# A hybrid attention and DeltaNet layer: the products P V of a head pair in one visit, the relative bias in float32r, and new stream delays

## The chip, the core and the metric

The kernel runs on one core of a Trainium2 chip. The metric is the device time in microseconds (us) of one execution; smaller is better. The engines are named as in the profile: PE (TensorE, matmuls and transposes), PEld (its weight loads), DVE (VectorE), ACT (ScalarE), POOL (GpSimd) and SP (SyncE, which issues most transfers).

## The reference

One decoder layer with 512 tokens and width 1024, all in float32. Eight heads of block-sparse attention and eight heads of a gated DeltaNet work side by side on one input projection; their outputs share one output projection; an MLP with a squared ReLU follows. Cut to what matters:

```python
h = rms_norm(x, pre_mix_norm)
proj = h @ w_in                       # 512x1024 by 1024x(3*512 + 3*512 + 512 + 16)
att_q, att_k, att_v, gdn_qkv, gdn_z, gdn_a, gdn_b = split(proj)

# attention, 8 heads of 64: own block of 256 keys (causal) and the past block
l = q k^T / 8 + rel_bias[:, rel_bucket(q_pos - k_pos)]     # -inf where not visible
p = softmax(l);  o_att = p v
# rel_bucket(d): d below 16, else 16 + log-spaced up to 31; rel_bias is 8 x 32

# gated DeltaNet, 8 heads of 64, chunks of 64 tokens
q, k, v = silu(causal_conv4(gdn_qkv)); q, k l2-normalised
u, w = triangular_solve(I + strict_lower(beta k k^T * decay), [beta v, beta k e^g])
for each chunk:                        # a scan over 8 chunks with a 64x64 state
    v_new = u - w S;  o = q S + (q k^T * decay) v_new;  S = S e^g_last + k^T v_new
o_gdn = rms_norm(o) * norm_w * silu(z)

x = x + rms_norm([o_att, o_gdn] @ w_out, post_mix_norm)
m = square(relu(rms_norm(x, pre_mlp_norm) @ w_up)) @ w_down     # 1024 -> 4096 -> 1024
out = x + rms_norm(m, post_mlp_norm)
```

## The kernel before, in words

**Arithmetic.** A float32 product of the projections is made from three float32r passes: each operand is split in a high part (`_h`, `_hi`: the value rounded to float32r) and the remainder (`_l`, `_lo`), and `mm3` issues high x high, high x low and low x high. Rows `ps_mm<-hT_h,w_hi`, `hT_l,w_hi`, `hT_h,w_lo` are such passes of 512 columns with the transposed, normed input `hT` and a chunk of `w_in`. A chunk `w_raw` comes by a transfer of SP (256 KB), ACT makes `w_hi` of it (L154), and POOL or DVE makes `w_lo` (L155). `LO_DVE = (26, 40)` names the chunks whose `w_lo` is DVE's.

**Streams and their order.** The front of the layer is written as generators: `projections` (the spine, whose items `k0 q0 x0 k1 ...` stand in the string `ORDER`; k, q, v, z are parts of the DeltaNet, x and y queries and keys of the attention, w the attention's values), `pre_norm`, `constants_in`, `bias`, `scalars`, `chunks(p)`, `inverse`, `scan`, `scores`, `values`, `finish_o(t)`, `weights_out`, `output` and others. A class `Weave` runs them. It keeps a virtual time `now` which each matmul advances by its columns / 2400 us (four times that in float32), and always continues the first stream, in rank order, whose start has come. A stream gives way with `yield wait["name"]` (so many us later) or `yield "mark"` (when another stream has set that mark). `WAIT` and `SINGLE` hold those delays, per name or per occurrence, `RANK` and `LEAD` the ranks and priorities, `START` some first starts. The order on PE is exactly the order in which the generators issue; the other engines' queues are set in issue order at first and by the tile scheduler later, with `LEAD` as priority. Each engine works through its own list in order, so PE waits where its next instruction's operand or bank is late. A second part, from the attention's end on (output projection, norm, MLP), follows.

**Banks.** PSUM has eight banks of 128x512, by tag: two `mm` (projections), three `g` (DeltaNet) and three `a` (attention). A row's `ps_a` is a bank of tag `a`.

**Attention.** The heads go in four pairs p = 0..3. `scores` (from L682) makes for each block of 128 queries, q = 3, 2, 1, 0, the scores of both heads in two `a` banks (`ps_a<-pt`), DVE adds the bias read from `E` and keeps the smallest (L708), ACT takes the exponential into `L` (L710) and sets the mark `row{p}{q}` later. The inverses of the row sums are copied to `R` (L715), with a mark `sums{p}`. `values` (L720 to L770) handles one pair after another. `block(k)` transposes the parts of `L` that belong to key block k on PE (L101, `ps_a<-ident,L`) into `a` banks and copies them to `ph` on ACT (L736). `product(k, P)` adds P V of that key block, two heads side by side on the PE columns (128x64 tiles, `ps_a<-ph,V`), into the bank `po`; key block k has 512 - 128 k columns, and each product is four records in the trace. The order in a pair is: block 3, take bank `po`, then block 2, product 3, block 1, product 2, product 1, block 0, the transposes of `R` into a bank `rb` (copied to `t` by ACT, L762), product 0, and the scaling. Between those steps the stream yields, so projection passes or DeltaNet work stand between.

**Relative bias.** `bias_in` (L197) loads a one-hot table `hot` (33 x 640: bucket by distance; row 32 is the mask row) and `rel_bias` into `rb` (33 x 8). `bias` (L651) multiplies them in float32 on PE in two matmuls (512 and 128 columns; `ps_a<-L,rb`), copies the 8 x 640 result with its sign changed into `es` and stores it to DRAM, from where `scores` reads each head's row as a sliding window.

**DeltaNet.** k and q go through a convolution on ACT and DVE (L409, L412, L416) and are transposed on PE (`ps_g<-ident,kraw`); sums of squares become rsqrt factors by a power on POOL (`rstd_of`, L188 and L192, tile `by`). `inverse` works on DVE, and `scan` joins it: the merge is two runs of 32x32 matmuls (`uap,NT` and `UT,uap`), then 64x64 ones (`UT,kB`), then eight scan steps (`S,LWQ`, `vn,kdec`, `vn,AT`). `finish_o(t)` norms a token tile's output and transposes it (`ps_g<-ident,ot`), and DVE scales it into `om` (L933). `weights_out` loads the 16 chunks `wo_raw` of the output projection; `output` uses them (`wo_h,mg_h`).

Of the kernel before, what the change touches and what calls it, by code (L numbers as in the profile page):

```python
# [85 lines left out]
def layer(ctx, tc, nc, x, w_in, w_v, w_ab, w_out, w_up, w_down, conv_w, a_log, dt_bias, gdn_norm_w, rel_bias,  # L86
          pre_mix, post_mix, pre_mlp, post_mlp, c_ident, c_mask, c_tri, c_ones, c_sel, c_su, c_hot, out):
    stt = nc.vector.scalar_tensor_tensor
    tt = nc.vector.tensor_tensor
# [4 lines left out]
    ctx.enter_context(tc.manual_schedule(engines={mybir.EngineType.PE}))

    def mm(o, l, r, **kw):
        nc.tensor.matmul(o, l, r, **kw)  # L97
# [97 lines left out]
    rel = []  # L195

    def bias_in():  # L197
        he = at.tile([128, 1280], FT, name="L")
# [3 lines left out]
        nc.vector.memset(rb, -1e30)
# [517 lines left out]
    def values():  # L720
        for p in range(4):
            yield f"row{p}3"
            yield "v"

            def block(k):
                w = 512 - 128 * k
                P = []
                for hs in (((0, 1),) if k > 1 else ((0,), (1,))):
                    tp = bank("a")
                    for i, hh in enumerate(hs):  # L730
                        for q in range(k, 4):
# [4 lines left out]
                    nc.scalar.copy(pt[:, :n], tp[:, :n])  # L736
# [25 lines left out]
            nc.scalar.copy(rs, rb)  # L762
# [771 lines left out]
```

## Time and profile before

| | us |
|---|---|
| median of 3 runs (lowest to highest) | 632.41 (632.14 to 632.89) |
| span of the profiled execution | 634.2 |
| PE busy | 622.9 |
| DVE, ACT, POOL busy | 443.7, 359.4, 157.9 |

The profiled execution's time is that span, 634.2 us; the runs without the profiler are the metric. In the profile's rows, a time is in us from the start of the span; `x4` counts records; `128*64 128x256` is a PE tile of 128 rows and 64 columns with 256 columns of moving data; `[0.29 <-ACT ph L736]` says that the engine had been idle 0.29 us and what ended that. A name in front of `<-` is written, those behind it are read. PE's matmuls overlap, so the step from one start to the next is what a matmul costs.

### The profile page before, as it was taken

How to read it: one execution, taken by the hardware profiler on the slowest of the kernel's cores; microseconds unless marked ns; L12 is line 12 of the kernel's file. 1: busy time of each engine (PE TensorE's matmuls, PEld its weight loads, DVE VectorE, ACT ScalarE, POOL GpSimd, SP SyncE). 2: the span in 40 equal slices, each digit the busy share in tenths (PEclk: the TensorE clock that was granted, in tenths of full speed). 3: DMA queues.
4: the chain of work that ended last, by engine and by line, in shares of the span. 5: the costliest groups of instructions: out<-in, count | busy, mean ns of one | idle time of the engine just before them, and what ended most of it. 6: DMA issues, size and time to landing. Idle time of an engine off the chain costs nothing.

```text
span 634.2 us, 11129 instructions
## 1 busy us (share of the span) xinstructions
PE 622.9 (98%) x4359; PEld 524.1 (83%) x4359; DVE 443.7 (70%) x635; ACT 359.4 (57%) x610; POOL 157.9 (25%) x197
## 2 busy tenths in 40 slices
PE   8999999999999999999999999999999999999995
PEld 6877777877876777688998999999998888888884
DVE  4456667599724464658665678878789888887776
ACT  6366586254387548654225586566765656665661
POOL 4346555500234343004212311111130320000001
PEclk9999999999999999999999999999999999999999
DMA  7222332422731112563488899999999999867503
GB/s 247 78 90 83 84 109 76 128 88 71 186 94 52 36 35 82 188 229 132 162 336 233 159 276 268 228 241 286 270 264 340 310 291 285 270 213 283 198 1 132
DMA packets 60629, 113.16 MB, mean 178 GB/s; under 512 B 15734, under 2 KB 35321, under 8 KB 60194
## 3 DMA queue, kind: packets, MB, share of 16 engines
q1 hardware_dynamic: 42876, 83.09, 37.8%
q0 software_dynamic: 17696, 29.36, 22.2%
q8 instruction: 34, 0.56, 0.3%
q14 instruction: 17, 0.14, 0.1%
q10 hardware_dynamic: 6, 0.00, 0.0%
HBM read 106.65 MB, written 35.15 MB: 224 GB/s over the span
## 4 chain that ended last, share of the span: by engine, by line
PE 91%; DVE 3%; DMA 2%; ACT 2%; POOL 1%; issue 0%; POOLq 0%; DVEq 0%; SPq 0%; ACTq 0%
PE ps_mm L97 46%; PE ps_g L97 26%; PE ps_a L97 16%; PE ps_a L101 2%; PE ps_g L101 1%; DMA wo_raw<-in_w_out 1%; DMA xx<-in_x 1%; DVE conv L412 1%; DMA w_raw<-in_w_in 0%; DVE wo_l L143 0%; POOL w_lo L155 0%; POOL oss L192 0%; DVE hT_l L131 0%; POOL by L192 0%; DVE xs L249 0%
## 5 line engine op out<-in xcount | busy, mean ns | idle before, releaser
L130 ACT CAST wdh<-wd 128x1024 fp32r<-128x1024 f32 x53 | 55.9, 1054 | 51.4 <-PE ps_mm L97 22.6
L131 DVE TENSOR_TENSOR u_l<-w,u_h 128x1024 fp32r<-128x1024 f32 x46 | 56.2, 1224 | 37.3 <-ACT u_h L130 37.1
L131 DVE TENSOR_TENSOR wdl<-wd,wdh 128x1024 fp32r<-128x1024 f32 x53 | 64.9, 1224 | 22.2 <-ACT wdh L130 22.1
L130 ACT CAST u_h<-w 128x1024 fp32r<-128x1024 f32 x46 | 47.9, 1046 | 56.8 <-DVE w L1177 15.6
L97 PE MATMUL ps_mm<-hT_h,w_hi 128*128 128x512 f32 (+1 forms) x192 | 79.4, 413 | 0.0
L97 PE MATMUL ps_mm<-hT_l,w_hi 128*128 128x512 f32 (+1 forms) x192 | 74.6, 388 | 0.3 <-DVE hT_l L131 0.3
L97 PE MATMUL ps_mm<-hT_h,w_lo 128*128 128x512 f32 (+1 forms) x192 | 74.5, 388 | 0.0
L155 POOL TENSOR_TENSOR w_lo<-w_raw,w_hi 128x512 fp32r<-128x512 f32 x40 | 51.8, 1297 | 77.2 <-ACT w_hi L154 67.4
L1210 POOL DMA_DIRECT2D d_T<-in_w_down x32 | 33.0, 1033 | 143.8 <-DMA d_T<-in_w_down 82.4
L154 ACT CAST w_hi<-w_raw 128x512 fp32r<-128x512 f32 x56 | 34.6, 620 | 52.9 <-PE ps_mm L97 17.5
L97 PEld LDWEIGHTS ps_mm<-hT_h,w_hi 128*128 128x128 f32 x192 | 37.1, 193 | 11.3 <-issue 4.8
L97 PE MATMUL ps_mm<-wdh,u_h 128*128 128x512 f32 x116 | 45.2, 390 | 0.0
L97 PE MATMUL ps_mm<-wdl,u_h 128*128 128x512 f32 x116 | 45.1, 389 | 0.0
L97 PE MATMUL ps_mm<-wdh,u_l 128*128 128x512 f32 x116 | 45.1, 389 | 0.0
L97 PEld LDWEIGHTS ps_mm<-hT_h,w_lo 128*128 128x128 f32 x192 | 37.2, 194 | 7.5
L97 PEld LDWEIGHTS ps_mm<-hT_l,w_hi 128*128 128x128 f32 x192 | 37.3, 194 | 6.0 <-DVE hT_l L131 0.6
L412 DVE SCALAR_TENSOR_TENSOR conv<-ps_mm,cw,conv 128x511 f32<-128x511 f32 (+2 forms) x36 | 26.8, 745 | 11.3 <-ACT conv L409 11.0
L131 DVE TENSOR_TENSOR u_l<-f,u_h 128x1024 fp32r<-128x1024 f32 x28 | 34.1, 1217 | 0.0
L708 DVE CUSTOM_DVE_ANT_0 L<-ps_a,E 128x512 f32<-128x512 f32 (+3 forms) x32 | 14.4, 489 | 23.9 <-PE ps_a L97 23.7
L97 PE MATMUL ps_g<-wdh,u_h 128*128 128x512 f32 x80 | 31.1, 389 | 0.0
L97 PE MATMUL ps_g<-wdl,u_h 128*128 128x512 f32 x80 | 31.1, 389 | 0.0
L97 PE MATMUL ps_g<-wdh,u_l 128*128 128x512 f32 x80 | 31.1, 389 | 0.0
(452 smaller groups left out, 1761.3 us busy)
## 6 DMA issues: line engine op xcount, KB each, us to landing
d_T<-in_w_down POOLq DMA_DIRECT2D x48, 512.0 KB, 11.6
wd<-d_T SPq DMA_DIRECT2D x32, 512.0 KB, 6.2
w<-in_w_up SPq DMA_DIRECT2D x28, 512.0 KB, 8.0
wd<-in_w_down SPq DMA_DIRECT2D x24, 512.0 KB, 7.7
w_raw<-in_w_in SPq DMA_DIRECT2D x46, 256.0 KB, 2.7
wo_raw<-in_w_out SPq DMA_DIRECT2D x16, 256.0 KB, 3.4
d_T<-d_T POOLq DMA_DIRECT2D x8, 512.0 KB, 12.7
xx<-in_x SPq DMA_DIRECT2D x4, 512.0 KB, 6.4
```

Of the source, the lines that this page charges most:

```text
L97: nc.tensor.matmul(o, l, r, **kw)
L101: nc.tensor.transpose(o, i, ident[:k, :k])
L130: nc.scalar.copy(hi, src)
L131: tt(lo, src, f32(hi), op=OP.subtract)
L154: nc.scalar.copy(hi, raw)
L155: (sub or tt)(lo, raw, f32(hi), op=OP.subtract)
L412: stt(c[:, s:], p[:, :512 - s], cw[:, ft, j:j + 1], c[:, s:], op0=OP.mult, op1=OP.add)
L708: nc.vector.tensor_tensor_reduce(out=l, in0=s[hh][:, :w], in1=Es[hh][:, w - 1::-1], scale=1.0, scalar=3e38, op0=OP.add, op1=OP.min, accum_ ...
L1210: nc.gpsimd.dma_start(d_T[t][k], block(b, second)[k], accum_op=OP.add, max_dma_last_dim=1024)
```

## The change

**P V.** In `values` a pair's four blocks are transposed first, k = 3, 2, 1, 0, each when its mark `row{p}{k}` has come; `ph` has 8 buffers instead of 4. Then come the transposes of `R`, the wait `pv0`, and only then the bank `po` and all four products in a row.

**Bias.** The constant `hot` is 128 x 640 with the table in rows 0 to 32 and again in 64 to 96, zero elsewhere; it is loaded after `rel_bias`. POOL casts it to float32r (`hot_r`, in the second buffer named `L`), ACT writes the high part of `rb` into rows 0 to 32 of `rs`, DVE the remainder into rows 64 to 96 (the rest is set to zero), so that one float32r pass sums high and low part. That preparation waits for the mark `h3` (the fourth token tile has been transposed) and the delay `bias`.

**Delays.** All tables have other numbers, `SINGLE` has many more entries, q1 and q2 and the order of v0 to v3 change places in `ORDER`, and `LO_DVE` is (33, 46). The counts of matmuls are the same but for the bias.

The diff (tables cut to a line or two):

```diff
-WAIT = {'h': 1.7, 'conv_k': 5.5, ..., 'wo': 0.97, 'wo_out': 17.6, ..., 'pv0': 1.53}
+WAIT = {'h': 0.99, 'conv_k': 5.48, ..., 'wo': 5.9, 'wo_out': 26.28, ..., 'pv0': 4.65, 'bias': 0.77}
...
-ORDER = "k0 q0 x0 k1 q1 q2 y0 k2 k3 z0 q3 x1 w0 v0 v1 v2 v3 y1 x2 y2 x3 y3 z1 z2 z3"
-LO_DVE = (26, 40)
+ORDER = "k0 q0 x0 k1 q2 q1 y0 k2 k3 z0 q3 x1 w0 v1 v3 v2 v0 y1 x2 y2 x3 y3 z1 z2 z3"
+LO_DVE = (33, 46)
...
     def bias_in():
         he = at.tile([128, 1280], FT, name="L")
-        hot, es = he[:33, :640], he[:8, 640:]
-        nc.sync.dma_start(hot, c_hot)
+        hot, es = he[:, :640], he[:8, 640:]
         rb = at.tile([33, 8], FT, name="rb", bufs=1)
         nc.vector.memset(rb, -1e30)
         nc.sync.dma_start(rb[:32], rel_bias)
-        return hot, es, rb
+        nc.sync.dma_start(hot, c_hot)
+        rs = at.tile([128, 8], FR, name="rs", bufs=1)
+        nc.vector.memset(f32(rs), 0.0)
+        return hot, es, rb, rs
...
     def bias():
-        hot, es, rb = rel
+        hot, es, rb, rs = rel
+        hot_r = at.tile([128, 1280], FT, name="L")[:, :640].bitcast(FR)
+        yield "h3"
+        yield wait["bias"]
+        nc.gpsimd.tensor_copy(hot_r, hot)
+        nc.scalar.copy(rs[:33], rb)
+        tt(rs[64:97], rb, f32(rs[:33]), op=OP.subtract)
         yield max(0, START[4] - weave.now)
         for a, b in ((0, 512), (512, 640)):
             pe = bank("a")
-            mm(pe[:8, :b - a], rb, hot[:, a:b], start=True, stop=True)
+            mm(pe[:8, :b - a], rs, hot_r[:, a:b], start=True, stop=True)
...
-                    pt = at.tile([128, 512], FT, name="ph", bufs=4)
+                    pt = at.tile([128, 512], FT, name="ph", bufs=8)
...
-            P = block(3)
-            po = bank("a")
+            P = {3: block(3)}
             for k in (2, 1, 0):
                 yield f"row{p}{k}"
-                if k > 0:
-                    N = block(k)
-                yield wait["pv"]
-                product(k + 1, P)
-                if k == 0:
-                    N = block(0)
-                P = N
+                P[k] = block(k)
             mark(f"turned{p}", wait["turned"])
...
             yield wait["pv0"]
-            product(0, P)
+            po = bank("a")
+            for k in (3, 2, 1, 0):
+                product(k, P[k])
```

What this does to the engines' lists is seen at three places. First, PE in pair 0, from the last transposes of `R` and `L` to the P V products; before, the products of key blocks 2 and 1 and their surroundings:

```order
L97 MATMUL ps_mm<-hT_h_83,w_lo 128x512
L97 MATMUL ps_a<-ph,V 64x256 x2
L97 MATMUL ps_mm<-hT_h_82,w_hi 128x512
L97 MATMUL ps_mm<-hT_l_84,w_hi 128x512
L97 MATMUL ps_mm<-hT_h_82,w_lo 128x512
L97 MATMUL ps_a<-ph,V 64x384 x2
L101 MATMUL ps_a<-ident,L 128x128 x8
L101 MATMUL ps_a<-ident,R_1042 128x128 x4
L97 MATMUL ps_mm<-hT_h_82,w_hi 128x512
```

After, the transposes:

```order
L97 MATMUL ps_mm<-hT_h_82,w_lo 128x512
L101 MATMUL ps_a<-ident,L 128x128 x20
L101 MATMUL ps_a<-ident,R_1069 128x128 x4
L97 MATMUL ps_mm<-hT_h_82,w_hi 128x512
L97 MATMUL ps_mm<-hT_l_84,w_hi 128x512
```

and, 21 projection passes later, the products:

```order
L97 MATMUL ps_mm<-hT_h_83,w_lo 128x512
L97 MATMUL ps_a<-ph,V 64x128 x2
L97 MATMUL ps_a<-ph,V 64x256 x2
L97 MATMUL ps_a<-ph,V 64x384 x2
L97 MATMUL ps_a<-ph,V 64x512 x2
L97 MATMUL ps_mm<-hT_h_82,w_hi 128x512
```

All 20 transposes of `L` and the four of `R` are now one group, and the four products another. Second, PE in pair 1, where the merge of the inverse, the P V products and the first scores of pair 2 (`ps_a<-pt`) meet; before:

```order
L97 MATMUL ps_g<-uap,NT 32x32 x64
L97 MATMUL ps_a<-ph,V 64x128 x2
L101 MATMUL ps_a<-ident,L 128x128 x6
L97 MATMUL ps_g<-UT,uap 32x32 x64
L97 MATMUL ps_a<-ph,V 64x256 x2
L97 MATMUL ps_a<-ph,V 64x384 x2
L101 MATMUL ps_a<-ident,L 128x128 x8
L97 MATMUL ps_g<-UT,kB 64x64 x16
L101 MATMUL ps_a<-ident,R_2025 128x128 x4
L97 MATMUL ps_a<-pt 128x512 x6
L97 MATMUL ps_g<-UT,kB 64x64 x16
L97 MATMUL ps_a<-ph,V 64x512 x2
```

After:

```order
L97 MATMUL ps_g<-uap,NT 32x32 x64
L101 MATMUL ps_a<-ident,L 128x128 x8
L101 MATMUL ps_a<-ident,R_2030 128x128 x4
L97 MATMUL ps_g<-UT,uap 32x32 x64
L97 MATMUL ps_a<-pt 128x512 x6
L97 MATMUL ps_a<-ph,V 64x128 x2
L97 MATMUL ps_a<-ph,V 64x256 x2
L97 MATMUL ps_a<-ph,V 64x384 x2
L97 MATMUL ps_a<-ph,V 64x512 x2
L97 MATMUL ps_g<-UT,kB 64x64 x16
```

The second 32x32 run has moved between the transposes of `R` and the scores, and the products have come together behind the scores. Third, POOL between its casts of the constants (`picks`) and the first power for k (`by`, L188 and L192); before:

```order
L386 CAST picks<-ident 128x128
L155 TENSOR_TENSOR w_lo<-w_raw,w_hi 128x512 x4
L188 TENSOR_SCALAR by_100<-ssq 128x4x2
L192 TENSOR_TENSOR by_100<-by_100,mhalf 128x4x2
L155 TENSOR_TENSOR w_lo<-w_raw,w_hi 128x512
```

After:

```order
L388 CAST picks<-ident 128x128
L658 CAST L<-L 128x640
L155 TENSOR_TENSOR w_lo<-w_raw,w_hi 128x512 x5
L188 TENSOR_SCALAR by_100<-ssq 128x4x2
L192 TENSOR_TENSOR by_100<-by_100,mhalf 128x4x2
L155 TENSOR_TENSOR w_lo<-w_raw,w_hi 128x512
```

The cast of the table (L658) has come in, and five chunks instead of four stand ahead of the power.

More of the change, by code (lines that the diff above doesn't have):

```diff
@@ L18 @@
 EPS = 1e-6
-WAIT = {'h': 1.7, 'conv_k': 5.5, 'k': 5.19, 'conv_q': 6.15, 'q': 2.1, 'conv_v': 11.0, 'v': 6.02, 'z': 2.87, 'ab': 0.1, 'g': 11.93, 'scalars': 4.76, 'r_in': 0.65, 'r_out': 4.45, 'kk': 2.71, 'kk_out': 14.43, 'gl': 3.13, 'qk': 3.88, 'va': 0.83, 'a': 5.81, 'row': 1.38, 'rows': 5.12, 'pv': 1.54, 'att': 1.17, 'inverse': 1.23, 'merge': 11.0, 'p1': 2.8, 'p2': 1.7, 'w': 2.33, 'vn': 1.0, 'state': 1.21, 'o_in': 3.96, 'o': 3.73, 'wo': 0.97, 'wo_out': 17.6, 'normed3': 7.6, 'normed': 11.21, 'n': 1.7, 'up': 1.9, 'sums': 2.64, 'turned': 0.5, 'pv0': 1.53}
@@ L22 @@
-SINGLE = {('h', 0): 0.05, ('inverse', 6): 2.02, ('state', 6): 3.71, ('row', 5): 0.98, ('inverse', 18): 0.05, ('inverse', 25): 0.05, ('vn', 7): 0.05, ('pv', 2): 0.1, ('h', 1): 0.05, ('turned', 0): 0.9, ('conv_k', 0): 4.12, ('normed', 0): 10.21, ('wo', 1): 1.97, ('conv_q', 0): 8.0, ('inverse', 16): 1.63, ('state', 1): 1.57, ('row', 6): 0.38, ('conv_v', 1): 8.5, ('conv_q', 2): 7.0, ('conv_k', 1): 5.1, ('o_in', 1): 4.36, ('kk', 2): 2.03, ('h', 2): 0.85, ('rows', 2): 6.66, ('vn', 1): 0.75, ('pv', 4): 2.77, ('inverse', 0): 0.61, ('rows', 0): 5.52, ('pv', 6): 2.0, ('rows', 4): 0.1, ('conv_v', 0): 14.3, ('kk_out', 0): 11.93, ('gl', 0): 5.63, ('inverse', 27): 0.23, ('row', 12): 2.48, ('state', 0): 0.21}
@@ L24 @@
-RANK = {'chunks': 1, 'inverse': 3, 'scan': 3, 'scores': 5, 'values': 5, 'finish_o': 2, 'take': 4}
-LEAD = {'chunks': 0, 'inverse': 100, 'scan': 100, 'scores': 0, 'values': 100, 'finish_o': 0, 'take': 200, 'take_a': 100}
+WAIT = {'h': 0.99, 'conv_k': 5.48, 'k': 5.65, 'conv_q': 5.41, 'q': 2.85, 'conv_v': 11.04, 'v': 2.5, 'z': 2.38, 'ab': 5.21, 'g': 7.58, 'scalars': 7.45, 'r_in': 0.22, 'r_out': 3.39, 'kk': 3.95, 'kk_out': 21.17, 'gl': 5.7, 'qk': 2.58, 'va': 0.38, 'a': 5.09, 'row': 2.47, 'rows': 5.12, 'pv': 1.45, 'att': 3.93, 'inverse': 0.05, 'merge': 7.32, 'p1': 3.55, 'p2': 0.79, 'w': 1.77, 'vn': 1.0, 'state': 2.54, 'o_in': 4.39, 'o': 3.11, 'wo': 5.9, 'wo_out': 26.28, 'normed3': 16.96, 'normed': 12.84, 'n': 2.52, 'up': 1.02, 'sums': 2.36, 'turned': 0.42, 'pv0': 4.65, 'bias': 0.77}
@@ new lines @@
+SINGLE = {('inverse', 6): 2.02, ('state', 6): 3.66, ('row', 5): 0.98, ('inverse', 25): 0.05, ('vn', 7): 0.14, ('pv', 2): 0.1, ('normed', 0): 10.24, ('wo', 1): 0.05, ('conv_q', 0): 8.69, ('inverse', 16): 1.63, ('state', 1): 1.57, ('row', 6): 0.33, ('vn', 1): 0.75, ('pv', 4): 2.77, ('inverse', 0): 0.93, ('rows', 0): 6.08, ('pv', 6): 2.0, ('rows', 4): 0.22, ('conv_v', 0): 14.23, ('kk_out', 0): 4.37, ('inverse', 27): 0.23, ('row', 12): 2.48, ('state', 0): 0.05, ('vn', 4): 0.05, ('g', 0): 11.27, ('n', 1): 2.8, ('row', 9): 4.41, ('inverse', 20): 1.09, ('state', 4): 1.35, ('inverse', 28): 4.43, ('rows', 7): 8.76, ('w', 2): 2.04, ('kk', 0): 2.54, ('normed3', 0): 8.63, ('n', 2): 1.44, ('state', 5): 2.54, ('r_in', 3): 1.83, ('w', 3): 2.33, ('scalars', 0): 4.74, ('rows', 5): 4.36, ('row', 3): 4.63, ('n', 0): 5.62, ('z', 3): 0.05, ('inverse', 3): 1.71, ('inverse', 9): 4.8, ('state', 2): 3.37, ('o_in', 1): 1.66, ('ab', 0): 1.72, ('inverse', 12): 1.27, ('o_in', 0): 2.04, ('sums', 0): 1.83, ('r_in', 0): 0.83, ('q', 3): 4.02, ('wo', 9): 2.75, ('rows', 11): 4.94, ('r_in', 2): 0.05, ('up', 1): 2.35, ('k', 0): 6.39, ('row', 13): 2.25, ('inverse', 21): 0.68, ('pv0', 2): 1.9, ('up', 6): 0.71, ('up', 2): 1.8, ('z', 1): 1.9, ('rows', 9): 5.32, ('rows', 6): 4.96, ('row', 15): 2.64, ('row', 1): 1.47, ('a', 0): 4.5, ('att', 2): 0.05, ('wo', 14): 10.37, ('wo', 13): 5.87, ('r_out', 2): 4.4, ('rows', 8): 4.94, ('v', 0): 14.25, ('conv_k', 3): 5.47, ('up', 0): 0.82, ('att', 1): 1.03, ('conv_q', 3): 4.72, ('normed', 1): 13.89, ('rows', 1): 6.91, ('inverse', 2): 0.05, ('k', 1): 4.72, ('turned', 0): 0.05, ('vn', 3): 1.16, ('q', 2): 3.48, ('pv0', 1): 4.89, ('q', 0): 2.14, ('o', 3): 4.07, ('k', 3): 5.87, ('up', 5): 2.84, ('wo_out', 0): 19.54, ('inverse', 10): 0.9, ('merge', 0): 10.2, ('v', 2): 12.67, ('w', 0): 1.68, ('inverse', 19): 1.66, ('pv0', 0): 4.39, ('wo', 2): 1.79, ('z', 0): 0.05, ('inverse', 24): 1.39, ('a', 3): 5.72, ('wo', 11): 3.51, ('rows', 3): 6.28, ('inverse', 14): 0.15, ('att', 0): 3.37, ('row', 10): 2.37, ('conv_k', 0): 8.86, ('v', 3): 14.13, ('normed', 2): 12.25, ('z', 2): 0.05, ('row', 2): 2.64, ('kk', 1): 4.01, ('wo', 12): 3.29, ('r_in', 1): 0.05, ('turned', 3): 0.69, ('q', 1): 2.97, ('att', 3): 6.62, ('v', 1): 8.52, ('up', 3): 0.37, ('wo', 4): 4.12, ('gl', 0): 4.0, ('vn', 6): 1.14, ('sums', 1): 0.05, ('inverse', 4): 0.32, ('row', 8): 1.29, ('k', 2): 6.9, ('h', 1): 2.19, ('row', 14): 2.55, ('n', 3): 0.68, ('inverse', 1): 0.05, ('wo', 5): 6.26, ('r_out', 1): 5.83, ('conv_v', 2): 10.65, ('r_out', 3): 4.33, ('inverse', 13): 0.05, ('state', 7): 2.1, ('h', 2): 1.08, ('o', 2): 3.63, ('w', 1): 1.57, ('conv_q', 2): 5.4, ('bias', 0): 0.23, ('a', 2): 4.78, ('p2', 0): 0.05, ('rows', 14): 5.33, ('turned', 1): 0.4, ('r_out', 0): 4.58, ('row', 7): 2.28, ('sums', 3): 1.81, ('o', 0): 2.87}
@@ L26 @@
+RANK = {'chunks': 2, 'inverse': 5, 'scan': 3, 'scores': 4, 'values': 4, 'finish_o': 1, 'take': 4}
+LEAD = {'chunks': 50, 'inverse': 50, 'scan': 50, 'scores': 200, 'values': 100, 'finish_o': 300, 'take': 300, 'take_a': 200}
 FILL = (6, 2)
 AT_X = (3, 5)
-START = (5.5, 9.7, 18.5, 13.8, 30, 15.0)
-ORDER = "k0 q0 x0 k1 q1 q2 y0 k2 k3 z0 q3 x1 w0 v0 v1 v2 v3 y1 x2 y2 x3 y3 z1 z2 z3"
-LO_DVE = (26, 40)
+START = (7.33, 8.64, 16.11, 13.39, 30.84, 13.77)
+ORDER = "k0 q0 x0 k1 q2 q1 y0 k2 k3 z0 q3 x1 w0 v1 v3 v2 v0 y1 x2 y2 x3 y3 z1 z2 z3"
@@ L1498, in constants @@
     bucket = np.where(d < 16, d, np.minimum(large, 31))
-    hot = np.zeros((33, 640), f)
-    hot[bucket, 127 + d] = 1
-    hot[32, :127] = 1
+    hot = np.zeros((128, 640), f)
+    for o in (0, 64):
+        hot[o + bucket, 127 + d] = 1
+        hot[o + 32, :127] = 1
     return {"c_ident": np.eye(128, dtype=f), "c_mask": np.where((n % 64)[:, None] <= np.arange(64), 0, -1e30).astype(f), "c_tri": upper.astype(f),
```

## The prediction

> **What bounds the kernel now.** I read the page's busy times, slices and chain first, then the list of waits of TensorE (PE), then the timeline round each place that the diff touches. The page's rows:
>
> ```profile
> span 634.2 us, 11129 instructions
> ...
> PE 622.9 (98%) x4359; PEld 524.1 (83%) x4359; DVE 443.7 (70%) x635; ACT 359.4 (57%) x610; POOL 157.9 (25%) x197
> ...
> PEclk9999999999999999999999999999999999999999
> ...
> PE 91%; DVE 3%; DMA 2%; ACT 2%; POOL 1%; issue 0%; POOLq 0%; DVEq 0%; SPq 0%; ACTq 0%
> ```
>
> PE is busy 98% of the span at full granted clock and is 91% of the chain that ended last. What shortens PE's own work or its waits shortens the time, and nothing else does. The stretches table splits the span at the start of the MLP's unbroken matmuls (columns: stretch, length, busy us and records of PE, PEld, DVE, ACT, POOL, then clock, DMA share, GB/s):
>
> ```profile
> 317.50:627.70 310.20, 310.16 (x1899) 279.43 (x1897) 246.88 (x236) 181.50 (x222) 47.68 (x60) 1.00 0.87 247
> ```
>
> There PE waits for nothing, and the diff leaves this order of matmuls as it was. The result is decided in the first 317 us. PE's waits (total, times, longest; the three below 0.7 us that belong to the first loads left out):
>
> ```profile
> PE ps_g L97 <- DVE rb L202: 1.1, 1, 1.1
> PE ps_g L101 <- DVE kraw L416: 1.0, 1, 1.0
> ...
> PE ps_g L101 <- DVE om L933: 0.4, 1, 0.4
> ...
> PE ps_a L101 <- ACT ph L736: 0.3, 1, 0.3
> PE ps_a L97 <- ACT t L762: 0.2, 1, 0.2
> ```
>
> So waits are short, some 2 us beyond the start. Most of what can be won is inside "busy".
>
> **Part 1: P V in one visit.** Pair 0 in the timeline (start, busy, engine, line, operation, count of records):
>
> ```profile
> 135.31 0.44 PE L97 MATMUL ps_a<-ph,V 128*64 128x128 f32 x4
> 135.68 0.88 PE L101 MATMUL ps_a<-ident,L 128*128 128x128 f32 x6
> ...
> 138.57 0.65 PE L97 MATMUL ps_a<-ph,V 128*64 128x256 f32 x4
> 139.16 0.50 PE L97 MATMUL ps_mm<-hT_h,w_hi 128*128 128x512 f32 x1
> 139.50 0.40 PE L97 MATMUL ps_mm<-hT_l,w_hi 128*128 128x512 f32 x1
> ...
> 140.06 0.87 PE L97 MATMUL ps_a<-ph,V 128*64 128x384 f32 x4
> 140.86 1.09 PE L101 MATMUL ps_a<-ident,L 128*128 128x128 f32 x8
> 142.24 0.55 PE L101 MATMUL ps_a<-ident,R 128*128 128x128 f32 x3 [0.29 <-ACT ph L736]
> ```
>
> Matmuls overlap, so I take starts, not durations. A product (four records) takes 0.37 us with 128 columns (135.31 to 135.68), 0.59 with 256, 0.80 with 384: 0.213 for each 128 columns and 0.157 once. The three projection passes between two visits take 0.90 (139.16 to 140.06). The same passes in an unbroken run, from the chain, and two products that already stand together in pair 1:
>
> ```profile
> 562.38 21.76 PE ps_g L97 x96
> ...
> 187.58 1.30 PE L97 MATMUL ps_a<-ph,V 128*64 128x256 f32 x8
> 188.81 1.09 PE L101 MATMUL ps_a<-ident,L 128*128 128x128 f32 x8
> ```
>
> 21.76 / 96 = 0.227 a pass, so three are 0.68; the way back costs 0.22. Two products of 256 and 384 columns take 1.23 = 5 x 0.213 + 0.165: the second pays nothing fixed. A visit costs 0.157 + 0.227 = 0.384 beyond its columns, whatever it holds.
>
> All products together are one group, 16 products of four records:
>
> ```profile
> L97 PE MATMUL ps_a<-ph,V 128*64 128x128 f32 (+3 forms) x64 | 11.8, 453 | 0.0
> ```
>
> Columns and records stay. Before, by the program's order, the 16 products make 13 visits of their own (pairs 0 to 3: 4, 3, 2, 4) and two stand next to the scan's S matmuls, which have the same 128x64 shape; one visit holds two. After, three pairs have one visit and pair 2's stands next to the S matmuls: 10 visits fewer, 10 x 0.384 = **-3.8 us**. Lower end, if leaving is paid anyway: 10 x 0.157 = -1.6. The blocks' transposes come in other groups (28 visits for 24); by 135.68 to 136.31, 0.63 for six, they cost little on entry: +0.1.
>
> [...]
>
> **Part 2: the bias in float32r.** Before (first two rows) and the nearest float32r matmuls of a narrow tile:
>
> ```profile
> 33.72 1.24 PE L97 MATMUL ps_a<-L,rb 33*8 33x512 f32 x4
> 34.89 0.66 PE L101 MATMUL ps_g<-ident,kraw 128*128 128x128 f32 x4
> ...
> 22.09 0.40 PE L97 MATMUL ps_g<-hT_h,abw 128*32 128x512 f32 x1
> 22.50 0.42 PE L97 MATMUL ps_g<-hT_l,abw 128*32 128x512 f32 x1
> 22.76 0.40 PE L97 MATMUL ps_g<-hT_h,abw 128*32 128x512 f32 x1
> 22.99 0.39 PE L97 MATMUL ps_g<-hT_l,abw 128*32 128x512 f32 x1
> ```
>
> Before: 34.89 - 33.72 = 1.17. After: 640 columns at 0.23 per 512 are 0.29, and entering cost 0.41 - 0.23 = 0.18 there: 0.47, so **-0.7** (ends -0.9 without the entry, -0.5 with 0.18 on leaving too). The cost beside PE: the hot table is 128 rows instead of 33, a longer transfer that SP now issues behind rel_bias; a cast of 128x640 on POOL; a 33x8 cast on ACT; a memset and a subtraction of a few elements on DVE. POOL's cast, from the row
>
> ```profile
> 27.42 2.52 POOL L155 TENSOR_TENSOR w_lo<-w_raw,w_hi 128x512 fp32r<-128x512 f32 x2 [5.35 <-ACT w_hi L154]
> ```
>
> is 2.52 / 2 x 640 / 512 = 1.6 us. POOL had idled 5.35 us before that row and the cast stands there, so 0. If the table's transfer were late, five w_lo would queue behind the cast and PE behind them: up to 1 us.
>
> **Part 3: the new delays.** They only matter where PE waited or will wait. (a) k1:
>
> ```profile
> 51.58 0.40 PE L97 MATMUL ps_mm<-hT_h,w_lo 128*128 128x512 f32 x1
> 52.98 0.66 PE L101 MATMUL ps_g<-ident,kraw 128*128 128x128 f32 x4 [1.00 <-DVE kraw L416]
> ...
> 41.83 1.65 POOL L192 TENSOR_TENSOR by<-by,mhalf 128x8 f32<-128x8 f32 x1
> 43.45 1.29 POOL L155 TENSOR_TENSOR w_lo<-w_raw,w_hi 128x512 fp32r<-128x512 f32 x1
> ```
>
> PE lost 1.40 - 0.23 = 1.17. The w_lo at 43.45 stood behind the 1.65 us power on POOL; now it is ahead of it, and the transposes stand three passes (0.68) later on PE. 1.65 + 0.68 covers 1.17: **-1.15** (ends -1.2 and 0). Late next is the power, which the preparation of the scan's chunks needs. (b) The scores of pair 2:
>
> ```profile
> 191.04 0.50 PE L97 MATMUL ps_a<-pt 64*128 64x512 f32 x1
> 191.79 0.96 PE L97 MATMUL ps_a<-pt 64*128 64x512 f32 x5 [0.25 <-ACT t L762]
> ...
> 185.50 2.14 PE ps_g L97 x128
> ```
>
> The step from first to second score pass is 0.75 instead of about 0.2 (five take 0.96): 0.55 lost, waiting for the bank that ACT's copy `t` empties. In the new order the second run of 32x32 matmuls (2.14 us, last row) stands between the transposes that ACT copies and the scores: **-0.55**. (c) The wait for om (0.4 above): the four products, 10 x 0.213 + 0.16 = 2.3 us, now stand between the last two groups of those transposes: **-0.3**, with 0.1 left for the next link.
>
> (d) New waits. Pair 0's blocks are now 24 transposes in a row (about 2.6 us) over three banks, which only ACT empties:
>
> ```profile
> 136.27 0.86 ACT L736 COPY ph<-ps_a 128x384 f32<-128x384 f32 x2 [0.94 <-PE ps_a L101]
> 141.60 1.07 ACT L736 COPY ph<-ps_a 128x512 f32<-128x512 f32 x2 [1.96 <-PE ps_a L101]
> ```
>
> Copies take 0.43 and 0.54 each. Stepping bank by bank, the fifth group waits about 0.3; a w_hi cast in between makes it 1.1. I take 0.6, where before lost 0.5 at 142.24 (1.38 from 140.86 for eight transposes of 0.11): **+0.1**. Queued behind on PE are the projections. For the chains I can't step through (scan steps drawn together, last finish_o), an allowance of **+0.5**: ends 0, and 3 us if as much is lost again as in the old waits.
>
> [...] Here ACT copies alone, which speaks against the change; by the rows above that is 0.3 to 1.1 us at pair 0.
>
> Sum: -3.8 + 0.1 - 0.7 - 1.15 - 0.55 - 0.3 + 0.1 + 0.5 = **-5.8 us**. The profiled execution's 634.2 lies 1.8 above the median of the runs, 632.41; the difference is applied to the median: **626.6 us**.
>
> **Rivals.** *The products keep their fixed cost.* If each of the 12 further products paid its 0.157, 1.9 us of the 3.8 would be lost: 628.5. The pair at 187.58 speaks against it.
>
> *New waits eat the gain.* The copies at pair 0, or a scan step drawn in front of its operand: 3 us more than allowed, 629.6. For it: ACT's copies are as long as the transposes. Against it: the other pairs' blocks keep 32x32 or projection work between them.
>
> *The waits vanish altogether.* Without the allowances and with about 1.2 us of short gaps (scan, end of attention) gone too: 632.4 - 5.8 - 0.6 - 1.2 = 624.8.
>
> *Slower: the output projection's weights.* Place: start of the output projection. The chain of before passes through its loads:
>
> ```profile
> 257.25 2.97 DMA wo_raw<-in_w_out
> ...
> 261.43 0.50 PE L97 MATMUL ps_mm<-wo_h,mg_h 128*128 128x512 f32 x1
> ```
>
> That chunk lands at 260.2, and PE starts the projection at 261.4 (second row, timeline), so they are hardly early. If PE comes 5.8 us sooner and the loads keep their time, all is given back; if the new delay `wo` (5.9 instead of 0.97) puts two further loads of 3 us behind, it is slower: 632.4 + 1 to 4 us. It decides from 7.1 us of lateness on (5.8 + 1.3). Against it: on ACT six wo_h casts stand ahead of pair 3's copy `t` (eight before), but that copy now stands about 6 us of PE work before the output projection, room for the two others.
>
> **How the numbers follow.** About 0.2%, 1.3 us, is what can be told from no change. Chances: forecast (625.4 to 628) 0.59; fixed cost kept 0.06; new waits 0.15; waits vanish 0.10; weights late, ending slower 0.06, ending within 0.2% (with the larger part of the other losses) 0.04. Faster 0.90, same 0.04, slower 0.06. The range runs from below "vanish" to above "new waits": 624.2 to 630.2, which leaves out the last two and a little of each tail.
>
> **What would show it.** Right: four P V products in one row of 16 records each pair, 2.3 us start to start; projections from visit to visit at 0.227 a pass; the bias step at 0.5; no wait for kraw of 1 us and none for `t`; the MLP's first unbroken matmul some 6 us earlier, then the same 310.2 us. Wrong: P V rows above 2.5 us; new waits for ph, vn, om or wo_h in the list above 1 us each; the MLP starting no earlier.

## The result, and the profile after

The changed kernel is slower: 638.82 us (median of 6 runs, 637.40 to 641.58) against 632.96 (6 runs of the kernel before, 632.14 to 636.19). The ratio is 1.0085 with a 95% interval of 1.0057 to 1.0113, some 5.4 us. The forecast of 626.6 us, faster with 0.9, had the wrong sign.

The page of the changed kernel:

```profile
span 638.2 us, 11127 instructions
...
PE 619.1 (97%) x4357; PEld 524.1 (82%) x4357; DVE 451.3 (71%) x636; ACT 359.6 (56%) x611; POOL 161.8 (25%) x199
...
PEclk9999999998999999999999999999999999999999
...
PE 81%; DVE 9%; DMA 5%; ACT 1%; issue 1%; POOL 1%; SPq 0%; POOLq 0%; DVEq 0%; ACTq 0%
```

PE is busy 3.8 us less, but the span is 4 us longer. (That the 3.8 equals the prediction's number for the visits is chance: it holds every change and also the slow clock told below.) PE's part of the chain fell from 91% to 81%, and DVE's rose from 3% to 9%. One slice of the clock has an 8 that was not there. DVE is busy 7.6 us longer (443.7 before), with hardly any new work. The list of PE's waits, columns as before:

```profile
PE ps_mm L97 <- DVE inv L786: 2.8, 1, 2.8
PE ps_g L97 <- ACT mg_h L130: 1.7, 1, 1.7
PE ps_g L101 <- DVE ot L927: 1.5, 1, 1.5
PE ps_mm L97 <- DVE conv L414: 1.1, 1, 1.1
...
PE ps_g L101 <- DVE kraw L418: 0.4, 1, 0.4
```

The waits for `t` and for om are gone and the one for kraw is smaller, and four larger ones have come. The prediction's sum had a term for the place of one of them only: ot is the next link of the chain behind om (0.1) and part of the last finish_o (in the allowance of 0.5). The MLP is as it was (310.20 us of before, same columns):

```profile
320.20:630.40 310.20, 310.20 (x1899) 279.46 (x1897) 246.88 (x236) 181.64 (x222) 47.74 (x60) 1.00 0.87 248
```

**Which origin to compare from.** Each run's time is its span plus 1.8 us, so the profiled execution of before was one of 636.0, about 3 us above its median. The surplus lies in the first 22 us: the first `abw` matmul, at 22.09 us there, starts here at

```profile
19.12 0.40 PE L97 MATMUL ps_g<-hT_h,abw 128*32 128x512 f32 x1
```

and in the profiles of this study, also of kernels with the same start, it lies between 18.7 and 22.2. Starts counted from that row, from the timelines (us; the last two columns are experiments told below):

| from the first abw matmul to the | before | changed | LO_DVE (26, 40) | LO_DVE (26, 46) |
|---|---|---|---|---|
| first matmul of the merge | 160.0 | 164.4 | 158.0 | 158.3 |
| first of the output projection | 239.3 | 241.3 | 237.5 | 235.3 |
| first of the MLP's unbroken run | 295.4 | 301.1 | 296.5 | 294.8 |

5.7 us are lost up to the MLP: 4.4 before the merge, and 3.7 inside the output projection, with 2.4 won back between. **The first place** is PE's timeline during the inverse:

```profile
143.39 0.39 PE L97 MATMUL ps_mm<-hT_h,w_lo 128*128 128x512 f32 x1
144.88 0.47 PE L97 MATMUL ps_mm<-hT_h,w_hi 128*128 128x512 f32 x1 [1.10 <-DVE conv L414]
...
150.19 0.39 PE L97 MATMUL ps_mm<-hT_h,w_lo 128*128 128x512 f32 x1
153.34 0.47 PE L97 MATMUL ps_mm<-hT_h,w_hi 128*128 128x512 f32 x1 [2.76 <-DVE inv L786]
...
154.14 0.63 PE L97 MATMUL ps_mm<-hT_h,w_hi 128*128 128x512 f32 x1
154.57 0.63 PE L97 MATMUL ps_mm<-hT_l,w_hi 128*128 128x512 f32 x1
...
157.13 0.55 PE L97 MATMUL ps_mm<-hT_l,w_hi 128*128 128x512 f32 x1
157.52 0.40 PE L97 MATMUL ps_mm<-hT_h,w_lo 128*128 128x512 f32 x1
...
154.00:156.00 2.00, 2.00 (x7) 1.53 (x6) 1.97 (x5) 1.11 (x2) 0.00 (x0) 0.52 0.44 152
```

Each new projection item needs one of two `mm` banks, and three conv steps on DVE must have read it. PE stands still 1.1 and 2.76 us. (The releaser of the second is put down to inv; the conv step that reads the bank ends 0.15 us ahead of the matmul.) From 154.1 on, passes follow at 0.43 us instead of 0.227, for about 3.4 us: the granted clock had dropped (0.52 from 154 to 156, last row, from the stretches table). Together that is 1.2 + 2.9 + 1.7, some 6 us. Why the conv steps are late is seen on DVE, with POOL's rows below:

```profile
133.07 0.42 DVE L785 TENSOR_TENSOR pr<-inv 128x256 f32<-128x256 f32 x1
133.99 1.39 DVE L785 TENSOR_TENSOR pr<-inv 128x255 f32<-128x255 f32 x1
...
136.78 1.37 DVE L785 TENSOR_TENSOR pr<-inv 128x247 f32<-128x247 f32 x1
138.19 0.42 DVE L786 TENSOR_TENSOR inv<-inv,pr 128x247 f32<-128x247 f32 x1
...
133.64 1.46 POOL L155 TENSOR_TENSOR w_lo<-w_raw,w_hi 128x512 fp32r<-128x512 f32 x1 [3.61 <-ACT w_hi L154]
136.36 1.52 POOL L155 TENSOR_TENSOR w_lo<-w_raw,w_hi 128x512 fp32r<-128x512 f32 x1 [1.26 <-ACT w_hi L154]
```

A step of the inverse takes 0.42 us here (0.2 to 0.4 where it is narrower), and 1.39 when a w_lo of POOL runs beside it: the two long ones end at 135.38 and 138.15, just behind POOL's passes (135.10 and 137.88). There are eight such steps here, +7.5 us in all against 0.42 each. Before there were two, DVE's rows first:

```profile
121.34 1.30 DVE L783 TENSOR_TENSOR inv<-inv,pr 128x112 f32<-128x112 f32 x1
124.05 1.37 DVE L782 TENSOR_TENSOR pr<-inv 128x175 f32<-128x175 f32 x1
...
121.21 1.30 POOL L155 TENSOR_TENSOR w_lo<-w_raw,w_hi 128x512 fp32r<-128x512 f32 x1 [1.59 <-ACT w_hi L154]
123.93 1.29 POOL L155 TENSOR_TENSOR w_lo<-w_raw,w_hi 128x512 fp32r<-128x512 f32 x1 [1.42 <-ACT w_hi L154]
```

The new `LO_DVE` gives the w_lo of chunks 26 to 32 to POOL (and those of 40 to 45 to DVE, later), and the first seven are made during the inverse. The length of a long DVE step goes by the end of POOL's pass: the two of the changed kernel's rows end 0.28 and 0.27 us behind it, the two of before 0.13 and 0.20. By what mechanism isn't shown.

**The second place** is the start of the output projection (PE, then DVE, then ACT):

```profile
250.35 1.15 PE L97 MATMUL ps_g<-vn,AT 64*64 64x64 f32 x32
259.99 0.63 PE L101 MATMUL ps_g<-ident,ot 128*128 128x128 f32 x4 [1.51 <-DVE ot L927]
267.58 0.50 PE L97 MATMUL ps_g<-wo_h,mg_h 128*128 128x512 f32 x1 [1.72 <-ACT mg_h L130]
...
258.31 0.75 DVE L936 SCALAR_TENSOR_TENSOR om<-ps_g,nw,zs 128x512 f32<-128x512 f32 x1
259.16 0.69 DVE L927 TENSOR_TENSOR ot<-ot,oss 128x512 f32<-128x512 f32 x1
...
264.20 1.25 ACT L142 CAST wo_h<-wo_raw 128x512 fp32r<-128x512 f32 x2 [1.03 <-DMA wo_raw<-in_w_out]
266.92 0.61 ACT L130 CAST mg_h<-om 128x512 fp32r<-128x512 f32 x1
```

The last scan matmul now stands 10 us ahead of the output projection (19.5 before), and its chain to the last transposes takes 9.6 us. Then mg_h waits on ACT behind casts of weight chunks that wait for their transfers.

### The profile page after: what moved, and what is told of

Its sections match the earlier page's. It is cut to its first block, busy times and chain, and to the rows that moved or that the text cites. A ratio compares the mean times of both kernels' runs of the same rounds, so it can differ in the third digit from the quotient of the medians.

```text
span 638.2 us, 11127 instructions
## 1 busy us (share of the span) xinstructions
PE 619.1 (97%) x4357; PEld 524.1 (82%) x4357; DVE 451.3 (71%) x636; ACT 359.6 (56%) x611; POOL 161.8 (25%) x199
## 3 DMA queue, kind: packets, MB, share of 16 engines
q0 software_dynamic: 17696, 29.36, 22.1%
## 4 chain that ended last, share of the span: by engine, by line
PE 81%; DVE 9%; DMA 5%; ACT 1%; issue 1%; POOL 1%; SPq 0%; POOLq 0%; DVEq 0%; ACTq 0%
PE ps_mm L97 41%; PE ps_g L97 24%; PE ps_a L97 14%; DMA wo_raw<-in_w_out 3%; DVE pr L785 2%; DVE inv L786 2%; PE ps_a L101 1%; PE ps_g L101 1%; DVE wo_l L143 1%; DVE conv L414 1%; DMA w_raw<-in_w_up 1%; DMA inv<-d_n 1%; DMA xx<-in_x 1%; ACT wo_h L142 1%; DVE xs L251 0%
## 5 line engine op out<-in xcount | busy, mean ns | idle before, releaser
L131 DVE TENSOR_TENSOR wdl<-wd,wdh 128x1024 fp32r<-128x1024 f32 x53 | 64.9, 1224 | 22.2 <-ACT wdh L130 22.1
L155 POOL TENSOR_TENSOR w_lo<-w_raw,w_hi 128x512 fp32r<-128x512 f32 x41 | 54.0, 1322 | 66.8 <-ACT w_hi L154 62.1
L1412 POOL TENSOR_TENSOR s<-s,mhalf 128x1 f32<-128x1 f32 x4 | 2.2, 553 | 109.0 <-DVE s L1411 109.0
```

The lines of the kernel that those rows point to most:

```text
L131: tt(lo, src, f32(hi), op=OP.subtract)
L155: (sub or tt)(lo, raw, f32(hi), op=OP.subtract)
```

## The experiments

Twelve kernels; each ratio is to the kernel before on the same chip.

**1 and 2. Who makes the w_lo of chunks 26 to 32.** First `LO_DVE` alone back, in the changed kernel:

```diff
-LO_DVE = (33, 46)
+LO_DVE = (26, 40)
```

> The changed kernel with LO_DVE back at (26, 40), nothing else: the w_lo of input chunks 26 to 32 are made on DVE again and not on POOL; PE's order stays word for word the same. Theory A (DVE is late): in the trace of the changed kernel eight steps of the inverse on DVE take 1.3 to 1.4 us instead of 0.42 where a POOL w_lo runs beside them (two in the kernel before), the three conv steps that empty PE's bank come 4.7 us late, PE waits 1.1 and 2.8 us there and then runs 2.3 us longer at a lower clock. Without the collisions, with seven more w_lo of about 0.6 on DVE, the waits shrink to 0 to 2 us and the clock doesn't drop: 3 to 5 us faster than the changed kernel, 634 to 636. Theory B (PE is ahead of its operands by the new delays whatever DVE's steps cost): the same 637 to 640. Theory C (the loss is at the start of the output projection): the same.

634.92 us, ratio 1.0013 (0.9994 to 1.0032): 3.9 us less than the changed kernel (4.6 by the ratios). No wait for conv or inv is left in its list. Then the work is taken off both engines: a plain copy on ACT stands in for the remainder, which this kernel leaves out.

```diff
-load = ... None if LO_DVE[0] <= n < LO_DVE[1] else nc.gpsimd.tensor_tensor
+on_act = lambda lo, raw, hi, op: nc.scalar.copy(lo, raw)
+load = ... None if LO_DVE[0] <= n < LO_DVE[1] else on_act if n >= 26 and n < 33 else nc.gpsimd.tensor_tensor
```

> The changed kernel, with the w_lo of input chunks 26 to 32 written by ACT as a plain copy of the chunk instead of POOL's remainder: this part of the computation is left out, so neither POOL nor DVE has the work during the inverse. Theory A: the inverse's long steps go from eight to three, DVE gains about 5 us, PE's waits of 1.1 and 2.8 us and the 2.3 us of low clock go: 5 to 6.5 us faster than the changed kernel, 632 to 634. Theory B: 637 to 640. Theory C: 637 to 640.

634.04 us, ratio 0.9994 (0.9975 to 1.0013): 4.8 us less than the changed kernel (5.8 by the ratios), the upper edge of A's 632 to 634. Both fall where A put them and 2 to 3 us below the range of B and C. The second run also settles a rival: that the new assignment only puts the conv steps later in DVE's list. In the changed kernel the second three stand behind 57 to 59 of the inverse's 62 steps, in experiment 1 behind 49 to 51. Here they stand behind 58 to 60, no earlier than in the changed kernel, but only one step is long (1.25 us) and PE doesn't wait for them.

**3. The same entry in the kernel before.**

```diff
-LO_DVE = (26, 40)
+LO_DVE = (33, 46)
```

> The kernel before with LO_DVE = (33, 46) alone: w_lo of chunks 26 to 32 on POOL during the inverse, those of 40 to 45 on DVE; PE's order stays word for word. Theory A (POOL's two-operand pass stops DVE's): long steps of the inverse go from two to seven or more, each +0.95 us, the conv steps stand at step 48 of the inverse instead of 43, and PE waits there: 2 to 6 us slower than the kernel before (635 to 639). Theory B (the assignment is harmless, only PE's lead in the changed kernel made it cost): within 1 us of the kernel before.

641.52 us, ratio 1.0139 (1.0098 to 1.0180): 8 us slower, more than A's 2 to 6, with PE's order unchanged. Nine steps of the inverse are long (the longest of its two lines 1.49 and 1.52 us, 1.37 and 1.30 before), and the conv steps also stand later in DVE's list (behind 48 of the steps, 43 before); the 8 us hold both. From its timeline and the stretches table:

```profile
155.98 0.77 PE L97 MATMUL ps_mm<-hT_h,w_hi 128*128 128x512 f32 x1 [4.03 <-DVE conv L412]
...
152.00:154.00 2.00, 0.00 (x0) 0.00 (x0) 1.90 (x5) 0.00 (x0) 0.01 (x1) 1.00 0.32 129
...
156.00:158.00 2.00, 2.00 (x5) 1.61 (x6) 1.79 (x4) 0.71 (x2) 1.15 (x1) 0.50 0.66 193
```

The kernel before falls into the same hole: 4 us of wait, then a granted clock of 0.50. B is refuted: one entry of the tables is enough, without any other part of the change.

**4. Only the early chunks back**, `LO_DVE = (26, 46)` in the changed kernel.

> The changed kernel with LO_DVE = (26, 46): only the w_lo of chunks 26 to 32 go back from POOL to DVE, those of 40 to 45 stay on DVE as in the changed kernel. Theory A: the chunks of the inverse's time are the cause, so the same as with (26, 40): 634 to 636, no wait for conv or inv. If the six later chunks mattered, it would lie nearer to 637.

632.02 us, ratio 0.9972 (0.9954 to 0.9991), 2 us below A's range, 0.3% faster than the kernel before, and by ratios 1.1% (some 7 us) faster than the changed kernel. The early chunks are the cause of the wait at the inverse. With the six later ones on DVE it is 0.4% faster than experiment 1, which A had not foreseen. In the profiles that difference lies behind the merge: there experiment 1 has a gap of 0.58 us on PE and then a granted clock of 0.51 and 0.64 (184 to 188 us), and this kernel has neither. How the six chunks would lead to that isn't shown. The second step of the inverse by line (count, then min/median/max in ns; 185/375/1415 in the changed kernel):

```profile
L786 DVE TENSOR_TENSOR inv<-inv,pr x31: 184/359/425, 118.0 to 156.7; 128x31 f32<-128x31 f32 x2, 128x60 f32<-128x60 f32 x2, 128x87 f32<-128x87 f32 x2, 128x112 f32<-128x112 f32 x2
```

None of these is long any more; two of the other line (L785, longest 1.43 us) still are, beside w_lo of the attention's values. Of all kernels here this one has the lowest time.

**5 and 6. The halves of the change.** The new P V and bias with all old tables, and all new tables with the old P V and bias:

```diff
 # 5: the kernel before, with the new bias_in, bias, values and c_hot
-..., 'pv0': 1.53}
+..., 'pv0': 1.53, 'bias': 0.77}
 # 6: the kernel before, with the new WAIT, SINGLE, RANK, LEAD, START, ORDER, LO_DVE
```

> The kernel before with the new P V form and the new bias, all delays, ranks and orders as before. Theory A, in which forms gain and the delays lose: 2 to 4 us faster than before (629 to 631), since a visit less is worth about 0.2 to 0.38 us and the bias 0.9. Rival D (the form itself loses: the transposes in a row wait for ACT's copies and the products for the last of them): 632 to 636.

> The kernel before in P V and bias, with all new tables (delays, ranks, leads, starts, ORDER, LO_DVE). Theory A: the eight long steps of the inverse and PE's waits for a projection bank are there as in the changed kernel, and it is slower than the kernel before by 6 to 10 us (639 to 643). Rival D: the tables alone are within 2 us of the kernel before (631 to 635).

650.09 us, ratio 1.0245 (1.0213 to 1.0277), and 652.32 us, ratio 1.0274 (1.0237 to 1.0311). Theory A's numbers (629 to 631 and 639 to 643) were far off in both, and so were rival D's. The waits of the first (two lines) and of the second:

```profile
PE ps_g L97 <- ACT vn L890: 3.5, 2, 2.8
PE ps_g L101 <- DVE om L936: 3.2, 1, 3.2
...
PE ps_mm L97 <- DVE inv L783: 4.8, 1, 4.8
PE ps_g L101 <- DVE om L933: 3.2, 1, 3.2
```

In the first, PE waits in the scan and at its end, where the diff changed nothing. The likely reason, read from the program and not tested: matmuls that are issued elsewhere move the virtual time, and by it every later choice of a stream. So these two runs don't price the forms and the delays apart; a comparison by parts needs kernels that keep PE's order. The second has the wait of the inverse again.

**7. What the visits cost.** In experiment 1's kernel, three projection passes between each two products of pair 0, one execution:

```diff
             for k in (3, 2, 1, 0):
                 product(k, P[k])
+                if k and p == 0:
+                    yield 0.3
```

> The changed kernel with LO_DVE = (26, 40), and in pair 0 three projection passes between each two of the four products: three visits more than in the one visit, between projection passes on both sides. By the price of the prediction 3 x 0.384 = 1.15 us more from the first product of pair 0 to the passes behind the last; if a visit costs only the 0.157 on entry, 0.47; if it costs nothing, 0.

```profile
137.95 0.44 PE L97 MATMUL ps_a<-ph,V 128*64 128x128 f32 x4
...
143.38 0.50 PE L97 MATMUL ps_mm<-hT_h,w_hi 128*128 128x512 f32 x1
```

From the first product to the passes behind the last: 5.43 us, of which nine passes at 0.227 are 2.04. The rest, 3.39, stands against 2.30 for the one visit: 1.09 for three visits, 0.36 each, near the 0.384. (Its one time, 641.1, tells nothing of three visits: its start was 2.5 us longer, the later order moved a little, and the clock dropped at two places instead of one.)

**8. The old bias** in experiment 1's kernel, with PE's order kept:

```diff
 # bias_in, c_hot and the rest of bias as in the kernel before; in the loop
-            mm(pe[:8, :b - a], rs, hot_r[:, a:b], start=True, stop=True)
+            mm(pe[:8, :b - a], rb, hot[:, a:b], start=True, stop=True)
+            weave.now -= 3 * (b - a) / 2400
```

> The changed kernel with LO_DVE = (26, 40) and the old float32 bias (PE's order otherwise kept, the virtual time too). The bias step took 1.17 us before and 0.29 in the changed kernel: 0.9 us slower than with LO_DVE alone, 635.5 to 636.5, and the row of the bias shows 1.2 us instead of 0.3. Rival: POOL's cast of the table and the longer table transfer cost elsewhere what the pass saves, then the same 634.5 to 635.3.

```profile
31.13 1.24 PE L97 MATMUL ps_a<-L,rb 33*8 33x512 f32 x4
32.30 0.50 PE L97 MATMUL ps_mm<-hT_h,w_hi 128*128 128x512 f32 x1
```

1.17 us against 0.29 in the changed kernel (below), and 636.57 us, ratio 1.0044 (1.0024 to 1.0064), 1.6 us above experiment 1. The row shows the gain of 0.88 us; the two intervals overlap, so the whole time fits that gain but doesn't show its size, nor whether more comes with it.

**9 to 11. What is left at the output projection**, in experiment 1's kernel. Left out: the last tile's norm factor. Then a buffer of its own for om; then also a later transposition of the third tile:

```diff
 # 9: finish_o, last token tile only
-        nc.gpsimd.tensor_tensor(ss, ss, rq2[:, t], op=OP.mult)
-        r = rstd_of(ss, ss, 64)
-        nc.gpsimd.tensor_tensor(r, r, rq8[:, t], op=OP.mult)
+        r = ss
 # 10
-        m = tmp2("om").rearrange("p (a b) -> p a b", a=4)
+        m = at.tile([128, 512], FT, name="E").rearrange("p (a b) -> p a b", a=4)
 # 11: 10, and
-('normed', 2): 12.25
+('normed', 2): 15
```

> The changed kernel with LO_DVE = (26, 40), and the last token tile's norm factor in finish_o left out (its three or four small POOL steps, some 3.5 us in a chain of 9.6 us from the last scan matmul to the tile's transposes); PE's order is the same. Theory C (what is left of the loss is the chain behind the last scan step, which stands 10 us ahead of the output projection instead of 19.5): PE's wait for ot (2.0) goes and the one for mg_h (1.1) shrinks, 2 to 3 us faster than with LO_DVE alone: 632 to 633. Rival E (mg_h waits for the weight chunks that stand ahead of it on ACT and DVE): the wait for ot goes, but the one for mg_h grows by the same, 634 to 636.

> The changed kernel with LO_DVE = (26, 40), and om in a buffer of its own (two of the attention's E buffers, free by then) instead of the one it shares with osq; PE's order is the same. Theory C (the second token tile's mg_h is late because the oms of the four tiles go through one buffer): the waits for mg_h and mg_l (1.4) go, 0.7 to 1.5 us faster than with LO_DVE alone: 633.4 to 634.2. Rival E (ACT's wo_h casts that wait for their transfers hold mg_h back): the same 634.5 to 635.3.

> As the run before, and the delay of the third token tile's normed transposes raised from 12.25 to 15 us, which moves these eight transposes behind the 20 next groups of matmuls: the 0.7 us wait for xs should go, 632.7 to 633.5. If the next transposes or matmuls then wait for the same chain, no gain: 633.4 to 634.2.

634.15 us, ratio 1.0012 (0.9991 to 1.0033); 633.62, 0.9990 (0.9968 to 1.0012); 634.74, 1.0009 (0.9989 to 1.0028). None differs from experiment 1 (1.0013) by more than the intervals. In the third the wait for xs, which should have gone, grew from 0.6 to 1.7. In the lists of waits what went came back next door: without the norm factor

```profile
PE ps_g L101 <- DVE om L939: 0.9, 1, 0.9
PE ps_mm L97 <- DVE mg_l L131: 0.7, 1, 0.7
```

stand for ot 2.0 and mg_h 1.1, and with om's own buffer, mg_h is gone but

```profile
PE ps_g L101 <- DVE ot L927: 2.5, 1, 2.5
```

has grown by 0.5. Theory C's place is right and its size isn't shown; several chains end there within a microsecond.

**12. PE kept busy through the wait**, in the changed kernel:

```diff
+            if item is items[16]:
+                idle = bank("a")
+                for k in range(11):
+                    nc.tensor.matmul(idle, hT_h[0][:, 0, :128], hT_h[0][:, 1], start=True, stop=True)
             ps = bank("mm")
```

> The changed kernel with 11 projection-sized matmuls of 2.5 us, whose result nobody reads, in the place where PE waits 2.8 us for its bank (at 150.4 us of its profile). If the low clock after that wait (0.52 and 0.63 for 4 us) comes from PE's being idle, it stays at full speed: 1.5 to 2.3 us faster than the changed kernel, 636.5 to 637.3. If it comes from something else, the same 638.8 or slower.

640.57 us, ratio 1.0103 (1.0071 to 1.0134): no gain. Timeline and stretches table:

```profile
147.13 0.47 PE L97 MATMUL ps_mm<-hT_h,w_hi 128*128 128x512 f32 x1 [1.91 <-DVE conv L418]
154.28 2.65 PE L332 MATMUL ps_a<-hT_h 128*128 128x512 f32 x11
...
148.00:150.00 2.00, 2.00 (x7) 1.57 (x6) 1.97 (x4) 1.32 (x3) 1.71 (x1) 0.56 0.04 8
...
154.00:156.00 2.00, 2.00 (x10) 1.65 (x10) 2.00 (x5) 0.49 (x1) 0.00 (x0) 1.00 0.00 0
```

Here the first wait took 1.91 us instead of 1.1, and the clock dropped behind it; behind the filled one it didn't. That fits a drop caused by idling, but the low clock moved, and a second one came (mean of the execution 0.991, against 0.995 in the changed kernel; 0.78, 0.50 and 0.87 from 270 to 276, behind waits of 1.6 for ot and 1.6 for mg_h, where the changed kernel kept its full clock behind 1.5 and 1.7). So the test doesn't settle it.

## Why the prediction was wrong, point by point

**What bounds the kernel:** right for the kernel before. (The 1.8 us that the prediction reads between the profiled execution and the median is the difference between a span and a time; that execution's time, 636.0, lay some 3 us above the median. As only a difference was applied, the forecast stays the same.) That DVE, with 70%, had a stretch of its own in which it was full was not looked for: from 138 to 158 us it is busy 1.83 to 2.00 of each 2 us in the changed kernel, and 1.55 to 2.00 before, with PE hardly waiting.

**Part 1, visits (-3.8):** the one visit takes 2.30 us, as worked out. Rows of the changed kernel, P V first, then bias:

```profile
135.74 2.37 PE L97 MATMUL ps_a<-ph,V 128*64 128x128 f32 x16
138.04 0.50 PE L97 MATMUL ps_mm<-hT_h,w_hi 128*128 128x512 f32 x1
...
30.64 0.46 PE L97 MATMUL ps_a<-L,rs 128*8 128x512 f32 x2
30.93 0.45 PE L97 MATMUL ps_mm<-hT_h,w_hi 128*128 128x512 f32 x1
```

The price holds between projections (0.36, experiment 7). The count was too simple: the ten removed visits all save the 0.157, but not all of them let two runs of passes grow together, since many stood beside transposes or scan matmuls, where the way back is paid anyway: in the kernel before the first pass takes 0.34 us to the next behind a product (from 139.16), 0.34 behind scan matmuls (from 207.62) and 0.32 behind transposes (from 136.31), against 0.227 in a run. By the program's order there are 54 runs of passes for 59, so 10 x 0.157 + 5 x 0.227 = 2.7 is nearer, an estimate from these prices. A miss of 1.1 us.

**Part 2, bias (-0.7):** right, 0.29 us instead of 1.17 (-0.88); the entry cost of the abw rows isn't paid here.

**Part 3 (a) to (c):** the wait for `t` went (-0.55, right). Of the wait for kraw 0.4 is left (-0.6 instead of -1.15). The wait for om is gone from the list, but the next link of the same chain, ot, costs 1.5.

**Part 3 (d), the new waits (+0.1 and +0.5): the step that failed.** Pair 0's transposes cost what was said (one wait of 0.3 for ph). The rest, priced at 0.5, was 6 us at the inverse and 3.7 us inside the output projection. The allowance was set without walking DVE's list. The sum holds no term at all for the `LO_DVE` change: the prediction doesn't speak of the seven passes that go from a busy engine to an idle one, which prices them at nothing, although the trace of before already held two inverse steps of 1.30 and 1.37 us, the two beside a POOL w_lo. Where the sum has nothing the runs show a cost of 8 us for that entry in the kernel before (experiment 3), and in the changed kernel 4 to 5 us for the whole entry (experiment 1) and 7 for its early chunks (experiment 4): larger than every other term and of the other sign.

It is the largest part of the miss and not all of it. By the ratios the changed kernel lies 1.8% above the forecast; experiment 1 wins back 0.7% of that and experiment 4 1.1%. Most of the rest is inside the output projection: from its first matmul to the MLP's run it takes 56.1 us before, 59.8 changed and still 59.5 in experiment 4, with the same matmuls. Which single cause makes that stays open (experiments 9 to 11).

**The rivals:** *fixed cost kept* is refuted by the one visit of 2.30 us. *The waits vanish* did not come: old waits went and longer ones came. *New waits* was right in kind, but at pair 0 and 3 us in size. *Slower* named the output projection; there were losses there, but PE never waited for a weight: casts of late chunks held mg_h and om back on ACT and DVE. The deciding place was in none of them.

## What to carry to other kernels

Before work is moved to an idle engine, look in the trace for an instruction of the busy engine that runs longer than its twins, and at what ran beside it: an engine's idle share doesn't say what its work costs another engine (POOL was busy 25% of the changed kernel's span, and eight steps of DVE took 7.5 us longer beside its passes). When PE is made shorter, walk the list of every engine that frees its banks through the same stretch, for here the gain became a wait where DVE was nearly full (1.83 to 2.00 of each 2 us). A table of delays in virtual time belongs to one form of the code: a part swapped alone reorders everything behind it, so compare only kernels whose order is the same.

## What the runs showed of the hardware

- The inverse's long steps on DVE (two operands, in SBUF), each beside a w_lo of POOL, end 0.1 to 0.3 us behind POOL's pass in the kernel before and the changed one: steps of 0.3 to 0.42 us became 1.29 to 1.42 in the changed kernel. Eight such steps cost 7.5 us there; in experiment 3 the longest took 1.52. The same w_lo made on DVE takes 0.68 in its rows.
- After an idle time of PE of 1.7 us (experiment 4, at the wait for ot), 2.8 (changed kernel) and 4.0 us (experiment 3), the granted clock fell to about half (0.50, 0.52 and 0.50); in the changed kernel for some 3.4 us, which cost a further 1.7 us. But it stayed full after 1.5 (ot) and 1.7 us (mg_h) in the changed kernel and after the 2.0 us wait for ot in experiment 1, where it had dropped instead behind the merge's small matmuls with a gap of 0.58 us. So the length of one idle time doesn't decide it. What does isn't shown.
- The start, up to the first abw matmul, took 22.1 us in the profiled execution of before, 19.1 in that of the changed kernel and 18.7 in experiment 4's, so two traces are best compared from a row behind it.
